# The inverse norms of the attention keys: from diagonal products on TensorE to a transfer through DRAM

## The chip, the core and the metric

The kernel runs on one core of a Trainium2 chip. The metric is the device time of one execution in microseconds (us), the median of several runs. One profiled execution gives the trace. Its engines are PE (TensorE matmul), PEld (its weight loads), DVE (VectorE), ACT (ScalarE), POOL (GpSimd) and SP (SyncE, which here issues the loads and stores). Each engine works through its own instructions in a fixed order.

## What is computed

The reference is one layer with two parallel token mixers. The change sits in the second, latent attention with normed queries and keys:

```python
kv = (_rms(ckv, kv_a_norm) @ w_ukv).reshape(B, T, MLA_HEADS, MLA_NOPE + MLA_V)
k_nope, v = kv[..., :MLA_NOPE], kv[..., MLA_NOPE:]
k = jnp.concatenate([k_nope, broadcast(k_rope)], axis=-1)
k = _rms(k, k_norm)          # each key is divided by the root of its mean square
...
s = jnp.einsum('bqhd,bkhd->bhqk', q, k) * (MLA_QK ** -0.5)
p = jax.nn.softmax(s, axis=-1)
```

There are 8 heads, 512 latent and 256 context tokens, so 768 keys a head. The kernel leaves the keys unscaled in the score product and multiplies each column of the scores by the inverse norm of its key afterwards. For that the 768 inverse norms of a head must stand in every one of the 128 partitions.

## The kernel before

All work on the core is one program whose instructions a scheduler puts in order for each engine; within an engine that order is then fixed. In the stage of interest three strands share the engines. The last part of the first mixer, `gdn_chain(3)`, is a serial recurrence of small 128x128 products (lines L751, L766, L786, L802, L805 on PE, L758 `rho` and L794 `s` on DVE). `queries` and `operands` prepare a head: the products with `ckh`/`ckl`, their splits into a high and a low part (L927 on ACT, L928 on DVE), and transposes (L995, L999, L1007). `attention` computes the scores in eight groups a head: five products of 384 columns into a PSUM bank `d` (L184 to L186, L1034, L1035), of which there are two, then DVE's L1036, which multiplies by `rkb` and takes the row maximum. It empties the bank for the group after next. Then follow exponential, transposes (L1046) and the product with the values.

The operands of a head are computed while an earlier head's attention runs; only heads 0 and 1 (numbered here in order of use) are prepared before any attention. In `operands`, the sum of squares `ssk` of each key ends in L980 on DVE, and POOL raises it to the power -0.5 (`power`, L149): `rk`, 128 partitions x 6 blocks, so that key 128b+p has its inverse norm in partition p, column b. To bring it into all partitions, `rk` is split into two float32r parts (`rkr`: L189 on ACT, L190 on DVE), POOL multiplies the identity by each (`dg`, 128x768, L987), PE multiplies a matrix of ones by both (L1013: two products of 512 and two of 256 columns a head, in two PSUM banks from the rotation of `pbank`), and ACT copies the two banks into `rkb` (L1014).

SP issues the loads in order. The weights (`wchunk`, L177) go through four buffers `wf`, so each load waits until DVE has split an earlier one.

Of the kernel before, what the change touches and what calls it, by code (L numbers as in the profile page):

```python
# [7 lines left out]
F32 = mybir.dt.float32  # L8
F32R = mybir.dt.float32r
AF = mybir.ActivationFunctionType  # L10
ALU = mybir.AluOpType
# [4 lines left out]
P = 128  # L16
# [5 lines left out]
NT = NL + NC  # L22
# [56 lines left out]
def f32(ap):  # L79
    return ap.bitcast(F32)  # L80
# [3 lines left out]
def tile_layer(ctx, tc, I, out, stop=None, dbg=None):  # L84
    nc = tc.nc
    act = nc.scalar
    dve = nc.vector
    pool = nc.gpsimd
    pe = nc.tensor

    def bc(ap, shape):
        return ap.to_broadcast(shape)
# [4 lines left out]
    dr = ctx.enter_context(tc.tile_pool(name="dr", bufs=1, space=DRAM))  # L97
# [3 lines left out]
    def bank(tag):  # L101
        return ps.tile([P, 512], F32, tag=tag, name=tag, bufs=banks[tag])
# [21 lines left out]
    def M(n):  # L124
        lo, hi = MASKS[n]
        return (mk2 if n in EARLY else mk)[:, lo:hi]

    ident = M("ident")
# [15 lines left out]
    onesf = cst.tile([P, P], F32, name="onesf")  # L144
    pool.memset(onesf, 1.0)

    def power(out_ap, in_ap, n, half):
        e = expt[:, 1 if half else 0, 0:n]
        pool.tensor_tensor(out_ap, in_ap, e, ALU.pow)  # L149
# [15 lines left out]
    def wchunk(src, nk=KT, n=P, eng=dve, keep=None):  # L165

        step = min(nk, WN // n)
        res = []
        for k in range(0, nk, step):
            wf = wp.tile([P, WN], F32, tag="wf", name="wf", bufs=4)[:, :step * n]  # L170
            if keep is None:
                wh = wp.tile([P, WN], F32R, tag="wh", name="wh", bufs=3)[:, :step * n]
                wl = wp.tile([P, WN], F32R, tag="wl", name="wl", bufs=3)[:, :step * n]
            else:
                wh = keep.tile([P, WN], F32R, tag="kh", name="kh", bufs=2 * KEEP)
                wl = keep.tile([P, WN], F32R, tag="kl", name="kl", bufs=2 * KEEP)
            nc.sync.dma_start(wf.rearrange("p (k n) -> p k n", k=step), src[:, k:k + step])  # L177
            act.copy(wh, wf)  # L178
            eng.tensor_tensor(wl, wf, f32(wh), ALU.subtract)  # L179
            res += [(wh[:, n * i:n * i + n], wl[:, n * i:n * i + n]) for i in range(step)]  # L180
        return res

    def mm3(po, lh, ll, rh, rl, first, last):
        pe.matmul(po, lh, rh, start=first, stop=False)  # L184
        pe.matmul(po, lh, rl, start=False, stop=False)  # L185
        pe.matmul(po, ll, rh, start=False, stop=last)  # L186

    def split_sb(full, hi, lo):
        act.copy(hi, full)  # L189
        dve.tensor_tensor(lo, full, f32(hi), ALU.subtract)  # L190
# [229 lines left out]
    for b0, n in ((0, 4), (4, 2)):  # L420
        t = bank("t")[:, :128 * n]
# [32 lines left out]
    raw = gx.tile([P, NG + 2 * GAP], F32, name="raw")  # L454
# [439 lines left out]
    lp = lpool.__enter__()  # L894
# [3 lines left out]
    krow = rows[:, 192:384]  # L898
    ropec = rows[:, 384:640].rearrange("p (b n) -> p b n", b=4)
    ropes = rows[:, 640:896].rearrange("p (b n) -> p b n", b=4)  # L900
    onesr = lp.tile([P, P], F32R, name="onesr")
    act.copy(onesr, onesf)
    cqh = lp.tile([P, 3, NL], F32R, name="cqh")
    cql = lp.tile([P, 3, NL], F32R, name="cql")
    ckh = lp.tile([P, 2, NT], F32R, name="ckh")
# [2 lines left out]
    mr = mrpool.__enter__()  # L908
    krx = lp.tile([P, NT], F32R, name="krx")
    for src, th_, tl_, nk, w in ((d_cq, cqh, cql, 3, 128), (d_kv, ckh, ckl, 2, 256)):  # L910
        for c0 in range(0, src.shape[2], w):
            c = slice(c0, c0 + w)
            raw = wp.tile([P, WN], F32, tag="wf", name="raw", bufs=4)[:, :nk * w]
            raw = raw.rearrange("p (a b) -> p a b", a=nk)
            nc.sync.dma_start(raw, src[:, :, c])
            split_sb(raw, th_[:, :, c], tl_[:, :, c])
    raw = mr.tile([P, NT], F32, tag="dg", name="raw")
    nc.sync.dma_start(raw, d_kr)
    act.copy(krx, raw)
    dve.tensor_tensor(krx[64:128], raw[64:128], f32(krx[64:128]), ALU.subtract)  # L920
# [3 lines left out]
    mp = mpool.__enter__()  # L924

    def split_ps(src, hi, lo):
        act.copy(hi, src)  # L927
        dve.tensor_tensor(lo, src, f32(hi), ALU.subtract)  # L928
# [3 lines left out]
    def pbank(pr):  # L932
        turn[0] += 1
        return bank("tece"[turn[0] % 4] if pr else "tdd"[turn[0] % 3])
# [24 lines left out]
    def operands(pr, h, qs, late=False):  # L959
        qn, qr, sc = qs  # L960

        uk = wchunk(I["w_ukv"][2 * pr + h], 2, 256)
        kn = mr.tile([P, 6, P], F32, tag="kn", name="kn", bufs=2)
        v2 = gp.tile([P, 2, 6, P], F32R, tag="A", name="v2", bufs=2)
        ssk = mr.tile([P, 6], F32, tag="ssk", name="ssk", bufs=2)
        rk = mr.tile([P, 6], F32, tag="rk", name="rk", bufs=2)
        junk = mr.tile([P, 128], F32, tag="junk", name="junk2")
        for b2 in range(3):
            po = pbank(pr or late).rearrange("p (a n) -> p a n", a=2)
            for bb in range(2):  # L970
                c = slice(256 * b2 + 128 * bb, 256 * b2 + 128 * bb + 128)
                for k in range(2):
                    mm3(po[:, bb], ckh[:, k, c], ckl[:, k, c], *uk[k], k == 0, k == 1)
            bs = slice(2 * b2, 2 * b2 + 2)
            for bb in range(2):
                act.activation(junk, po[:, bb, 0:128], AF.Square, accum_out=ssk[:, 2 * b2 + bb:2 * b2 + bb + 1])
            split_ps(po[:, :, 128:256], v2[:, 0, bs, :], v2[:, 1, bs, :])
            dve.tensor_tensor(kn[:, bs, :], po[:, :, 0:128], bc(krow[:, 0:128].unsqueeze(1), [P, 2, P]), ALU.mult)
        dve.tensor_tensor(ssk, ssk, sskr, ALU.add)
        dve.tensor_scalar(ssk, ssk, 1.0 / 192, EPS, op0=ALU.mult, op1=ALU.add)  # L980
        power(rk, ssk, 6, False)
        dgs = []
        rks = [mr.tile([P, 6], F32R, tag=t, name="rkr", bufs=2) for t in ("rkh", "rkl")]
        split_sb(rk, *rks)
        for rr, tag in zip(rks, ("dg", "dgl")):
            dg = mr.tile([P, 6, P], F32R, tag=tag, name="dg")
            pool.tensor_tensor(dg, bc(ident.unsqueeze(1), [P, 6, P]), bc(f32(rr).unsqueeze(2), [P, 6, P]), ALU.mult)  # L987
            dgs.append(dg.rearrange("p a b -> p (a b)"))
        qh = mp.tile([P, NL], F32R, tag="qh", name="qh", bufs=2)
        ql = mp.tile([P, NL], F32R, tag="ql", name="ql", bufs=2)  # L990
        qrh = mp.tile([P, NL], F32R, tag="qrh", name="qrh", bufs=2)
        qrl = mp.tile([P, NL], F32R, tag="qrl", name="qrl", bufs=2)
        t = pbank(pr or late)
        for b in range(4):
            pe.transpose(t[:, 128 * b:128 * b + 128], qn[:, b, h, 0:128], ident)  # L995
        split_ps(t, qh, ql)
        t = pbank(pr or late)
        for b in range(4):
            pe.transpose(t[:, 128 * b:128 * b + 128], qr[:, h, b].rearrange("p a b -> p (a b)"), ident)  # L999
        split_ps(t, qrh, qrl)  # L1000
        kh = mp.tile([P, NT], F32R, tag="kh", name="kh", bufs=2)
        kl = mp.tile([P, NT], F32R, tag="kl", name="kl", bufs=2)
        for b0, n in ((0, 4), (4, 2)):
            c = slice(128 * b0, 128 * (b0 + n))
            t = pbank(pr or late)[:, :128 * n]
            for b in range(n):
                pe.transpose(t[:, 128 * b:128 * b + 128], kn[:, b0 + b, :], ident)  # L1007
            split_ps(t, kh[:, c], kl[:, c])
        rkb = mp.tile([P, NT], F32, tag="rkb", name="rkb", bufs=2)
        for b0, n in ((0, 4), (4, 2)):  # L1010
            t = pbank(pr or late)[:, :128 * n]
            for i, dg in enumerate(dgs):
                pe.matmul(t, onesr, dg[:, 128 * b0:128 * (b0 + n)], start=(i == 0), stop=(i == 1))  # L1013
            act.copy(rkb[:, 128 * b0:128 * (b0 + n)], t)  # L1014
        return qh, ql, qrh, qrl, kh, kl, rkb, v2[:, 0], v2[:, 1], sc

    def attention(pr, h, ops):
# [35 lines left out]

    qs = queries(0)
    o0 = operands(0, 0, qs)
    o1 = operands(0, 1, qs, True)
    attention(0, 0, o0)
    gdn_out(3, res3)
    with ahead():
        qs = queries(1)  # L1060
        o0 = operands(1, 0, qs)
# [313 lines left out]
```

## Time and profile before

| | us |
|---|---|
| median of 3 runs (1328.95 to 1334.19) | 1329.18 |
| the profiled execution | 1332.53 |
| its span in the trace | 1330.7 |

A row of the timeline gives start and duration in us, engine, line, operation, tile written `<-` tiles read, the shape, how many in a row, and in brackets how long the engine sat idle before it and what it waited for. "q" behind an engine's name (SPq, ACTq) is its sequencer issuing a transfer. The row of a window gives its length, then, for PE, PEld, DVE, ACT and POOL in this order, the busy time and the number of instructions, then TensorE's granted clock as a share of its full speed, the share of DMA engine time in use and GB/s. Matmuls overlap in the pipeline, so what one costs is the step from its start to the next one's start, and not its duration.

### The profile page before, as it was taken

The page shows a single profiled execution, that of the slowest core. Times are in us where ns is not written, and L with a number is a line of the kernel's source. Part 1 is how long each engine was busy: PE and PEld are TensorE (multiplying, and loading weights), DVE is VectorE, ACT ScalarE, POOL GpSimd, SP SyncE. Part 2 cuts the span into 40 slices and gives each one's busy share as a digit, 9 for nine tenths or more (in the row PEclk, how much of TensorE's full clock was granted, in tenths as well). Part 3 has the DMA queues.
Part 4 walks back from the last instruction along what each step waited for, and adds up shares of the span by engine and source line. Part 5 has one row for each costly group of instructions (what it writes and reads, how often), then busy time and mean ns, then how long its engine had stood idle before and what let it go on. Part 6 is the DMA issues. An engine that isn't in the chain of part 4 may idle for free.

```text
span 1330.7 us, 21029 instructions
## 1 busy us (share of the span) xinstructions
PE 1269.9 (95%) x7430; PEld 1112.8 (84%) x7430; DVE 867.2 (65%) x1861; ACT 648.2 (49%) x1666; POOL 278.5 (21%) x372
## 2 busy tenths in 40 slices
PE   5899899998999999989999999999999999999998
PEld 4798787887888888879899998888997888888886
DVE  4656798866688678747778788676885333333332
ACT  4557575336653675356667576323443242242331
POOL 0022423223410431113112221222041010010110
PEclk9999998988999999999999999999999999999999
DMA  9333225210233124441011013766452222222232
GB/s 359 112 110 88 56 71 128 94 41 9 88 103 104 49 76 120 123 143 60 14 46 37 9 40 131 266 209 249 173 177 95 95 95 95 95 96 95 96 112 86
DMA packets 97993, 141.20 MB, mean 106 GB/s; under 512 B 32736, under 2 KB 41952, under 8 KB 97760
## 3 DMA queue, kind: packets, MB, share of 16 engines
q1 hardware_dynamic: 68576, 127.27, 28.8%
q10 hardware_dynamic: 29312, 12.59, 3.8%
q8 instruction: 59, 0.97, 0.3%
q14 instruction: 46, 0.38, 0.1%
HBM read 124.23 MB, written 15.60 MB: 105 GB/s over the span
## 4 chain that ended last, share of the span: by engine, by line
PE 82%; DVE 7%; DMA 4%; ACT 4%; issue 1%; POOL 1%; SPq 0%; DVEq 0%; ACTq 0%; POOLq 0%
PE d L184 20%; PE d L185 20%; PE d L186 20%; DMA wm<-in_w_mod 2%; PE p L184 1%; PE c L766 1%; PE p L185 1%; PE p L186 1%; PE c L786 1%; PE p L1046 1%; PE c L751 1%; PE e L802 1%; DVE kT L471 1%; PE e L805 1%; PE t L487 1%
## 5 line engine op out<-in xcount | busy, mean ns | idle before, releaser
L178 ACT CAST wh<-wf 128x512 fp32r<-128x512 f32 (+2 forms) x292 | 177.1, 610 | 352.2 <-PE d L185 307.4
L179 DVE TENSOR_TENSOR wl<-wf,wh 128x512 fp32r<-128x512 f32 (+2 forms) x268 | 182.9, 686 | 164.2 <-ACT wh L178 161.5
L184 PE MATMUL d<-hTh,wh 128*128 128x512 f32 x384 | 156.2, 407 | 4.2 <-ACT raw L466 3.5
L185 PE MATMUL d<-hTl,wh 128*128 128x512 f32 x384 | 155.0, 404 | 0.0
L186 PE MATMUL d<-hTh,wl 128*128 128x512 f32 x384 | 154.0, 401 | 0.0
L184 PE MATMUL d<-ah,wh 128*128 128x512 f32 x256 | 100.7, 395 | 0.0
L185 PE MATMUL d<-al,wh 128*128 128x512 f32 x256 | 100.7, 395 | 0.0
L186 PE MATMUL d<-ah,wl 128*128 128x512 f32 x256 | 100.6, 395 | 0.0
L1233 POOL TENSOR_TENSOR a<-r 128x512 f32<-128x512 f32 (+1 forms) x36 | 37.1, 1033 | 269.2 <-ACT r L1231 264.8
L184 PEld LDWEIGHTS d<-hTh,wh 128*128 128x128 f32 x384 | 73.7, 192 | 19.8 <-ACT raw L466 5.0
L186 PE MATMUL d<-h2h,wl 128*128 128x512 f32 x224 | 87.4, 390 | 0.9 <-DVE wl L179 0.9
L185 PE MATMUL d<-h2l,wh 128*128 128x512 f32 x224 | 87.2, 389 | 0.0
L184 PE MATMUL d<-h2h,wh 128*128 128x512 f32 x224 | 87.2, 389 | 0.0
L186 PEld LDWEIGHTS d<-hTh,wl 128*128 128x128 f32 x384 | 73.7, 192 | 14.0
L185 PEld LDWEIGHTS d<-hTl,wh 128*128 128x128 f32 x384 | 73.9, 193 | 13.3
L179 POOL TENSOR_TENSOR wl<-wf,wh 128x512 fp32r<-128x512 f32 x24 | 36.2, 1510 | 133.3 <-ACT wh L178 133.3
L1272 DVE SCALAR_TENSOR_TENSOR x<-d,mcol,x 128x512 f32<-128x512 f32 x32 | 24.0, 751 | 61.5 <-PE d L186 61.5
L186 PEld LDWEIGHTS d<-ah,wl 128*128 128x128 f32 x256 | 48.1, 188 | 11.6
L184 PEld LDWEIGHTS d<-ah,wh 128*128 128x128 f32 x256 | 48.1, 188 | 11.5
L185 PEld LDWEIGHTS d<-al,wh 128*128 128x128 f32 x256 | 48.1, 188 | 11.5
L186 PEld LDWEIGHTS d<-h2h,wl 128*128 128x128 f32 x224 | 42.0, 188 | 10.1 <-DVE wl L179 1.4
L184 PEld LDWEIGHTS d<-h2h,wh 128*128 128x128 f32 x224 | 42.0, 188 | 8.7
(552 smaller groups left out, 3468.0 us busy)
## 6 DMA issues: line engine op xcount, KB each, us to landing
wf<-in_w_mi SPq DMA_DIRECT2D x64, 256.0 KB, 2.7
wf<-in_w_mo SPq DMA_DIRECT2D x64, 256.0 KB, 2.6
wf<-in_w_qkv SPq DMA_DIRECT2D x48, 256.0 KB, 2.8
wm<-in_w_mod SPq DMA_DIRECT2D x40, 256.0 KB, 5.4
wm<-in_w_mod SPq DMA_DIRECT2D x16, 512.0 KB, 9.0
wf<-in_w_gate SPq DMA_DIRECT2D x32, 256.0 KB, 2.7
wms<-in_w_mod SPq DMA_DIRECT2D x12, 512.0 KB, 8.5
wf<-in_w_z SPq DMA_DIRECT2D x16, 256.0 KB, 2.7
```

What stands on the lines that cost most here:

```text
L178: act.copy(wh, wf)
L179: eng.tensor_tensor(wl, wf, f32(wh), ALU.subtract)
L184: pe.matmul(po, lh, rh, start=first, stop=False)
L185: pe.matmul(po, lh, rl, start=False, stop=False)
L186: pe.matmul(po, ll, rh, start=False, stop=last)
L471: dve.scalar_tensor_tensor(dst, raw[:, o + i:o + i + n], convh[:, ch, i:i + 1], dst, ALU.mult, ALU.add)
L487: pe.transpose(t[:, 128 * q:128 * q + 128], src[:, c:c + 128], ident)
L751: pe.matmul(t[:, 0, h, :], kT[:, h, at(bs[d]):at(bs[d]) + 128], S_[d][:, h, :], start=True, stop=True)
L766: pe.matmul(t[:, 0, h, :], Em[d][:, h, :], rho[d][h], start=True, stop=True)
L786: pe.matmul(t[:, 0, h, :], kn[:, h, bs[d], :], y2[d][:, h, :], start=True, stop=True)
L1233: pool.tensor_tensor(a_, r, r, ALU.mult)
L1272: dve.scalar_tensor_tensor(x1[:, ot, :], po, mcol[:, 5, ot, 0:1], x1[:, ot, :], ALU.mult, ALU.add)
```

## The change

The split of `rk`, the two diagonal matrices, the four products and the two copies of each head are gone, with the matrix `onesr`. In their place SP writes `rk` to a small DRAM tensor, transposed, so that the 768 values lie in a row, and then reads this row into all 128 partitions. The tile `raw`, which shared a buffer with `dg`, has a buffer of its own name.

```diff
-    onesr = lp.tile([P, P], F32R, name="onesr")
-    act.copy(onesr, onesf)
...
-        dgs = []
-        rks = [mr.tile([P, 6], F32R, tag=t, name="rkr", bufs=2) for t in ("rkh", "rkl")]
-        split_sb(rk, *rks)
-        for rr, tag in zip(rks, ("dg", "dgl")):
-            dg = mr.tile([P, 6, P], F32R, tag=tag, name="dg")
-            pool.tensor_tensor(dg, bc(ident.unsqueeze(1), [P, 6, P]), bc(f32(rr).unsqueeze(2), [P, 6, P]), ALU.mult)
-            dgs.append(dg.rearrange("p a b -> p (a b)"))
+
+        d_rk = dr.tile([6, P], F32, tag="d_rk", name="d_rk", bufs=2)
+        nc.sync.dma_start(d_rk.rearrange("b p -> p b"), rk, allow_slow_non_contiguous=True)
+        rkb = mp.tile([P, NT], F32, tag="rkb", name="rkb", bufs=2)
+        nc.sync.dma_start(rkb, bc(d_rk.rearrange("b p -> (b p)").unsqueeze(0), [P, NT]))
...
-        rkb = mp.tile([P, NT], F32, tag="rkb", name="rkb", bufs=2)
-        for b0, n in ((0, 4), (4, 2)):
-            t = pbank(pr or late)[:, :128 * n]
-            for i, dg in enumerate(dgs):
-                pe.matmul(t, onesr, dg[:, 128 * b0:128 * (b0 + n)], start=(i == 0), stop=(i == 1))
-            act.copy(rkb[:, 128 * b0:128 * (b0 + n)], t)
```

The scheduler then orders the whole attention stage anew; before and behind it the order is as it was. Lines behind the change move up: L978 is L976, L980 is L978, L1007 is L1003, L1034 and L1035 are L1024 and L1025, L1036 is L1026, and the two transfers are L982 and L984. On SP the two transfers of each head stand among the weight loads; this is the difference for the first two pairs of heads (`in_w_uq` and `in_w_ukv` are weights of `queries` and `operands`):

```order
-L177 DMA wf<-in_w_uq 128x384 x3
+L177 DMA wf<-in_w_uq 128x384
+L982 DMA d_rk<-rk 128x6x1
+L984 DMA rkb<-d_rk 128x768
+L177 DMA wf<-in_w_uq 128x384
+L982 DMA d_rk<-rk 128x6x1
+L984 DMA rkb<-d_rk 128x768
+L177 DMA wf<-in_w_uq 128x384
 L177 DMA wf<-in_w_ukv 128x512 x2
```

Each write waits on SP behind one weight load, and the read waits for the write; the next weight load stands behind both.

On DVE, this is what stands between the last split of head 0's keys (`kl`) and its first product with `rkb` before the change:

```order
L928 TENSOR_TENSOR kl<-d,kh 128x256
L772 TENSOR_SCALAR y_6603<-c,bkd 128x128
L190 TENSOR_TENSOR rkr<-rk,rkr 128x6
L794 SCALAR_TENSOR_TENSOR s_6615<-s_6549,egl,c 128x128 x2
L813 TENSOR_TENSOR ob<-ob,e 128x2x128
L794 SCALAR_TENSOR_TENSOR s_6618<-s_6552,egl,c 128x128 x2
L758 SCALAR_TENSOR_TENSOR rho<-c,negc,vn 128x128 x4
L813 TENSOR_TENSOR ob<-ob,e 128x2x128
L772 TENSOR_SCALAR y_6663<-c,bkd 128x128
L1036 ISA pp,mx<-d,rkb 128x384
```

And this is the same place of the changed program:

```order
L926 TENSOR_TENSOR kl<-d,kh 128x256
L772 TENSOR_SCALAR y_6603<-c,bkd 128x128
L794 SCALAR_TENSOR_TENSOR s_6615<-s_6549,egl,c 128x128 x2
L813 TENSOR_TENSOR ob<-ob,e 128x2x128
L794 SCALAR_TENSOR_TENSOR s_6618<-s_6552,egl,c 128x128 x2
L1026 ISA pp,mx<-d,rkb 128x384
L1026 ISA mx 128x1
L758 SCALAR_TENSOR_TENSOR rho<-c,negc,vn 128x128 x2
L1026 ISA pp,mx<-d,rkb,mx 128x384
L1026 ISA mx 128x1
L758 SCALAR_TENSOR_TENSOR rho<-c,negc,vn 128x128 x2
```

The first product with `rkb` has moved ahead of four steps `rho` of the recurrence, which now queue behind it.

On PE, the program before went from the transposes of head 0's keys straight to the recurrence, and to its first score group, like this (`dg` are the diagonal matrices):

```order
L1007 MATMUL d<-mk,kn 128x128 x6
L766 MATMUL c<-rho,Em 128x128 x2
L802 MATMUL e<-s_6549,qT 128x128 x2
L805 MATMUL e<-y,Qm 128x128
L786 MATMUL c<-y_6597,kn 128x128 x2
L805 MATMUL e<-y,Qm 128x128
L786 MATMUL c<-y_6603,kn 128x128 x2
L751 MATMUL c<-s_6615,kT 128x128 x2
L1013 MATMUL t<-dg,onesr 128x512
L1013 MATMUL d<-dg,onesr 128x256
L184 MATMUL d<-kh,qh 128x384
```

In the changed program twelve products for head 1 (`ckh`, `ckl`; the last of them stands in the first row) come between, and the first score group comes sooner:

```order
L186 MATMUL t<-wh,ckl 128x256
L766 MATMUL c<-rho,Em 128x128 x2
L802 MATMUL e<-s_6549,qT 128x128 x2
L184 MATMUL d<-kh,qh 128x384
L185 MATMUL d<-kl,qh 128x384
L186 MATMUL d<-kh,ql 128x384
L1024 MATMUL d<-krx,qrh 128x384
L1025 MATMUL d<-krx,qrl 128x384
L805 MATMUL e<-y,Qm 128x128
L786 MATMUL c<-y_6597,kn 128x128 x2
L805 MATMUL e<-y,Qm 128x128
L184 MATMUL d<-kh,qh 128x384
```

Two score groups and the products for head 1 thus stand ahead of the third group, the first that needs a bank back from DVE.

## Rows read from the trace of the kernel before

**Rows 1.** The page: span, and busy time of the engines.

```profile
span 1330.7 us, 21029 instructions
PE 1269.9 (95%) x7430; PEld 1112.8 (84%) x7430; DVE 867.2 (65%) x1861; ACT 648.2 (49%) x1666; POOL 278.5 (21%) x372
```

**Rows 2.** Windows: the attention stage's first 10 us and the stage.

```profile
620.00:630.00 10.00, 8.64 (x64) 7.53 (x64) 7.29 (x25) 4.69 (x16) 6.14 (x8) 1.00 0.06 18
620.00:825.00 205.00, 195.70 (x1387) 185.62 (x1387) 159.92 (x482) 135.93 (x417) 47.26 (x38) 1.00 0.11 36
```

**Rows 3.** The stage's window for L1013 alone (PE, PEld), then L1014 alone (ACT).

```profile
620.00:825.00 205.00, 9.95 (x32) 5.41 (x32) 1.00 0.11 36
...
620.00:825.00 205.00, 7.09 (x16) 1.00 0.11 36
```

**Rows 4.** Timeline of PE around the last products of head 2's `rkb`.

```profile
692.45 0.39 PE L1013 MATMUL c<-dg,onesr 128*128 128x512 f32 x1
692.68 0.28 PE L1013 MATMUL e<-dg,onesr 128*128 128x256 f32 x1
692.79 0.33 PE L1035 MATMUL d<-krx,qrl 128*128 128x384 f32 x1
```

**Rows 5.** What PE waited for at L1013, and who waited for L1014.

```profile
  POOL dg L987: 0.6, 2
...
PE c L487 <- ACT rkb L1014: 0.6, 1, 0.6
```

**Rows 6.** Timeline, heads 0, 1, 2: POOL's `rk`, ACT's second copy into `rkb`.

```profile
622.38 1.32 POOL L149 TENSOR_TENSOR rk<-ssk,expt 128x6 f32<-128x6 f32 x1 [1.64 <-DVE ssk L980]
629.68 0.38 ACT L1014 COPY rkb<-d 128x256 f32<-128x256 f32 x1
654.84 1.32 POOL L149 TENSOR_TENSOR rk<-ssk,expt 128x6 f32<-128x6 f32 x1 [16.70 <-DVE ssk L980]
663.81 0.38 ACT L1014 COPY rkb<-c 128x256 f32<-128x256 f32 x1
685.33 1.32 POOL L149 TENSOR_TENSOR rk<-ssk,expt 128x6 f32<-128x6 f32 x1 [7.08 <-DVE sm L1041]
693.36 0.38 ACT L1014 COPY rkb<-e 128x256 f32<-128x256 f32 x1
```

**Rows 7.** DMA issues: KB each, median us from issue to landing.

```profile
wf<-in_w_ukv SPq DMA_DIRECT2D x8, 256.0 KB, 2.9
d_kv<-nres SPq DMA_DIRECT2D x6, 128.0 KB, 2.2
dA<-Da ACTq DMA_DIRECT2D x4, 192.0 KB, 3.0
rows<-in_rows SPq DMA_DIRECT2D x1, 448.0 KB, 3.1
d_kr<-krt SPq DMA_DIRECT2D x1, 384.0 KB, 4.3
raw<-d_kr SPq DMA_DIRECT2D x1, 384.0 KB, 5.4
```

**Rows 8.** Timeline of ACT's queue: a write to DRAM and the read that waits for it.

```profile
151.13 0.39 ACTq L600 DMA_DIRECT2D dA<-Da  x1
153.76 0.36 ACTq L610 DMA_DIRECT2D pt<-dA  x1
```

**Rows 9.** Timeline of SP and POOL: the weight load ahead of head 5, its `rk`.

```profile
744.33 0.33 SPq L177 DMA_DIRECT2D wf<-in_w_bg  x1
745.48 1.32 POOL L149 TENSOR_TENSOR rk<-ssk,expt 128x6 f32<-128x6 f32 x1 [8.63 <-PE d L1035]
```

**Rows 10.** Timeline of DVE ahead of head 0's first L1036.

```profile
625.61 0.60 DVE L794 SCALAR_TENSOR_TENSOR s<-s,egl,c 128x128 f32<-128x128 f32 x2
628.52 0.61 DVE L758 SCALAR_TENSOR_TENSOR rho<-c,negc,vn 128x128 f32<-128x128 f32 x2 [1.80 <-PE c L751]
629.82 0.56 DVE L1036 CUSTOM_DVE_ANT_0 pp<-d,rkb 128x384 f32<-128x384 f32 x1
```

More of the change, by code (lines that the diff above doesn't have):

```diff
@@ L916, in tile_layer @@
             split_sb(raw, th_[:, :, c], tl_[:, :, c])
-    raw = mr.tile([P, NT], F32, tag="dg", name="raw")
+    raw = mr.tile([P, NT], F32, tag="raw", name="raw")
     nc.sync.dma_start(raw, d_kr)
```

## The prediction

> **What bounds the kernel now.** I read the page first: PE is busy for 95% of the span, DVE for 65%, ACT and POOL for less [rows 1]. An average over the whole program says little about one stage, so the windows came next. In the attention stage, from 620 to 825 us, PE is busy for 195.7 of 205 us at full clock, DVE for 159.9, ACT for 135.9 and POOL for 47.3 [rows 2]. PE sets the time there. What it does less is gained, as long as it finds work; what another engine does less is gained only where PE waits for it, and there are just 9.3 us of idle PE to win back (205 - 195.7). 1.36 of these lie in the first 10 us, where head 0's keys get ready [rows 2]. Third, I took the timeline of each head from `rk` to `rkb`, and last the transfers of the same size, since the change puts a transfer into that path.
>
> **What is removed on PE.** Each of 8 heads loses four products, 32 in all. Their window says 9.95 us [rows 3], but that counts pipelined durations. By the steps from start to start, the 512-column product of 692.45 holds PE for 0.23 us and the 256-column one behind it for 0.11 [rows 4]. Sixteen of each give 16 x (0.23 + 0.11) = **5.4 us**. PE also waited 0.6 us for `dg` and 0.6 us for ACT to empty a bank of `rkb` [rows 5]; both waits lose their cause: **1.2 us**.
>
> **What is removed elsewhere.** ACT loses 7.1 us of copies [rows 3], POOL its 16 diagonals, DVE eight tiny splits. None of the three is the bound, so I count nothing for them; what covers this is PE, which is busy meanwhile. If ACT's relief shortens waits of PE, it does so out of the 8.1 us of idle time that are left (9.3 - 1.2). That is a rival below.
>
> **What is added: the path from `rk` to `rkb`.** Before, it ran from the end of POOL's `rk` to the end of ACT's second copy. Head 0: 622.38 + 1.32 = 623.70 to 629.68 + 0.38 = 630.06, so 6.4 us. In the same way 8.0 us for head 1 (656.16 to 664.19) and 7.1 for head 2 (686.65 to 693.74) [rows 6]. Heads 4 and 6 repeat head 2. These five have their first use close behind; heads 3, 5 and 7 have more time.
>
> Now it is a write, a wait, and a read. No data transfer of the trace writes 4-byte pieces, so the write is bounded by others. `d_kv` writes 256 pieces of 512 bytes and lands in 2.2 us; `dA` writes 1536 pieces of 128 bytes (128 partitions x 12 columns) and lands in 3.0 [rows 7]. From the issue of `dA` to that of the read that waits for it there are 153.76 - 151.13 = 2.6 us [rows 8]. Here there are 768 pieces, between the two, and I take 2.6 to the issue of the read; the slowest write in the list, `d_kr`, took 4.3. The read brings 128 rows of 3 KB, 384 KB: 256 KB take 2.9, 448 KB take 3.1, but `raw<-d_kr`, which has exactly this shape, took 5.4 [rows 7]. I take 3.5, nearer to the first two, because the transfers of this stage are few (0.11 of the DMA engines' time, [rows 2]). That all 128 rows come from the same 3 KB of DRAM occurs nowhere before; it is the part that I know least. Sum: 2.6 + 3.5 and about 0.1 to wake SP is **6.2 us**; ends: 2.2 + 2.9 = 5.1 and 4.3 + 5.4 = 9.7. Against 6.4, 8.0 and 7.1 before, `rkb` comes no later than it did.
>
> A rule of the Trainium skill speaks against this write: "DMA: Bandwidth & Descriptors", section "Rules for kernel authors", says that a strided last dimension becomes one descriptor per element, and that transposing by a plain DMA with a rearranged access pattern is 19 times worse than the hardware's transpose. The rows above show no such price down to 128 bytes: 1280 pieces more cost 0.8 us. If each 4-byte piece nonetheless cost 19 times that, 768 of them would take 9 us (an estimate from that page's factor); the five close heads would be late by some 8 us each, and at full price the kernel would take about 1329 + 40 - 7 = 1362 us.
>
> **SP's queue.** The write waits on SP for `rk`, and the read for the write; weight loads queue behind for about 2.7 us. They are issued far ahead of their use, so this costs nothing. The other way round, the write must not wait behind a weight load that has no free buffer. The closest case before is 744.33 for the load against 746.80 for the end of `rk` [rows 9]: 2.5 us of room. DVE's new order keeps the same number of weight splits ahead of each head's sums, so I count nothing. If that cover went, the head would be late by what the load is late.
>
> **The new order.** Head 0 is where it can cost. DVE finishes `s` at 626.21, and its next instruction is now the product with `rkb` [rows 10], which at 623.70 + 6.2 = 629.9 starts as it did before (629.82). DVE stands still for 3.7 us, against 1.80 before. Behind it queue the four `rho` of the recurrence, of which the first two had run at 626.12; PE's L766 waits for them, so the recurrence is set back by up to 4 us. PE itself has two score groups and the twelve products for head 1 to do meanwhile, and would have done those later anyway. By the time the bank comes free it is ahead in attention and behind in the recurrence. Between nothing and the 3.7 us I take **1 us** of PE time lost, nearer to nothing because of that work. Head 1's first product with `rkb` also stands only a few splits behind its sums, and I take **1 us** for it too. Later heads have more PE work ahead of the group that needs a bank: nothing.
>
> **Sum.** -5.4 - 1.2 + 1 + 1 = **-4.6 us**. Against its own execution, that is 1332.53 - 4.6 = 1327.9. That execution lies 3.35 us above the median of the runs (1329.18), so the forecast is 1329.2 - 4.6 = **1324.6 us**. A measurement of this kernel can tell a change of about 0.5%, 6.6 us, from none.
>
> **Rivals.**
> - *The gain is used up* (1329, from 1327 to 1335). DVE waits for `rkb` at five heads, and PE runs dry behind it. If each is late by 1.3 us at full price, 5 x 1.3 = 6.5 us eat the 5.4 + 1.2. For it: the two bounds of the path differ by 4.6 us, and the first use followed the copies at once. Against: 6.2 is below what the path took before.
> - *More is gained* (1320.6). ACT's 7.1 us go out of the stage in which PE's splits, exponentials and bank copies wait for it, and half of the 8.1 us of other idle time closes: -4.6 - 4 = -8.6. Against: the new order was not made by these waits, and DVE still does 150 us or more of work.
> - *The transfer is slow* (1340, slower). The 4-byte pieces or the 128 reads of one row take what the two `d_kr` transfers took, 9.7 us. Then the path is 3.5 us longer than forecast at each of five close heads: 17.5 us at full price, less 6.6: +10.9. It decides from about 2.7 us of lateness a head on, a path of some 9 us. The page's 19-fold rule is the same mechanism at a higher price. For it: no row shows such pieces. Against: pieces of 128 bytes were cheap.
> - *The change does nothing on PE*, because the products had filled idle time: 1329, counted with the first. PE's 95% in this stage speaks against it.
>
> **Chances.** The forecast (1322.6 to 1327) has 0.36, the gain used up 0.21, more gained 0.28, the slow transfer 0.15. Faster by over 0.5% is therefore 0.28, within 0.5% 0.36 + 0.21 = 0.57, slower 0.15. The range leaves out the slow case and a little of the best: 1316 to 1336. The forecast's own range is 1322.6 to 1327, on the fast side of no change.
>
> **What would show it.** In the changed kernel's profile: PE's busy sum in the stage falls by about 10 us in durations, while the stage's length falls by 4 to 5. `d_rk` lands in 2.2 to 3 us and `rkb` in 3 to 4. DVE waits for the transfer at its first product with `rkb` of heads 0 and 1 for 2 to 4 us, and at later heads for 2 or less. The weight loads behind the transfers are on time. The prediction is wrong if `rkb` lands over 8 us after `rk`, if a write sits behind a weight load, or if PE's idle time in the stage changes by more than 4 us either way.

## The result and the profile after

The changed kernel takes 1380.02 us (median of 6 runs, 1377.56 to 1384.53), the kernel before on the same chip 1330.12: a ratio of 1.0374, with a 95% interval of 1.0349 to 1.0399. The change costs 50 us where 4.6 were to be gained. The prediction was wrong.

The page of the changed kernel, its span, engines and clock in 40 slices, to set beside [rows 1]:

```profile
span 1381.4 us, 20968 instructions
PE 1277.1 (92%) x7398; PEld 1117.2 (81%) x7398; DVE 865.3 (63%) x1853; ACT 641.1 (46%) x1641; POOL 254.6 (18%) x356
...
PEclk9999999999999999988899898999999999999999
```

PE has 32 products fewer and is yet busy for 7.2 us longer than before; the share of the span falls from 95% to 92%. Each digit of the clock's row stands for 34.5 us. The first 8 lies ahead of the attention stage and is not the change's doing: the kernel before has a stretch of half clock at the same place, as a window of its trace shows (its clock, 0.53, is the third figure from the end):

```profile
593.30:603.60 10.30, 8.54 (x34) 7.95 (x34) 6.01 (x12) 4.84 (x10) 0.41 (x1) 0.53 0.68 220
```

The other digits of 8 lie in the attention stage, where the kernel before had full clock [rows 2].

The transfers, and what the queue of SP and DVE waited for between 600 and 890 us (us in total, times, longest), beside [rows 7]:

```profile
d_rk<-rk SPq DMA_DIRECT2D x8, 3.0 KB, 10.2
rkb<-d_rk SPq DMA_DIRECT2D x8, 384.0 KB, 4.0
...
SPq L984 <- DMA d_rk<-rk: 76.8, 8, 11.0
...
DVE pp L1026 <- DMA rkb<-d_rk: 56.6, 7, 13.1
```

The smallest transfer of the program, 3 KB, is the slowest of these: it lands after 10.2 us, and the read of 384 KB behind it after 4.0. DVE stands still for it at seven of the eight heads. The path of head 0, on POOL, SP, DVE and PE, beside [rows 6] and [rows 10]:

```profile
623.05 1.32 POOL L149 TENSOR_TENSOR rk<-ssk,expt 128x6 f32<-128x6 f32 x1 [1.64 <-DVE ssk L978]
624.40 0.38 SPq L982 DMA_DIRECT2D d_rk<-rk  x1
635.29 0.33 SPq L984 DMA_DIRECT2D rkb<-d_rk  x1
638.82 0.56 DVE L1026 CUSTOM_DVE_ANT_0 pp<-d,rkb 128x384 f32<-128x384 f32 x1 [10.44 <-DMA rkb<-d_rk]
639.44 0.69 PE L184 MATMUL d<-kh,qh 128*128 128x384 f32 x1 [9.92 <-DVE mx L1026]
```

SP issues the write as soon as `rk` is there, the read 10.9 us later, and DVE starts 3.5 us behind that: 14.4 us from the end of `rk` (624.37), where it was 6.1 before (629.82 - 623.70, [rows 6, 10]). PE has filled both banks, and its third score group waits for 9.9 us. At the last head it is the same, as the chain that ended last shows (start, length, what):

```profile
842.90 10.12 DMA d_rk<-rk
853.03 5.00 DMA rkb<-d_rk
858.17 0.56 DVE pp L1026
858.79 0.69 PE d L184
```

What the DMA engines do meanwhile tells a window of head 0's write (length, then busy time and instructions of PE, PEld, DVE, ACT and POOL, the clock, the DMA share, GB/s):

```profile
626.00:635.30 9.30, 3.52 (x29) 3.33 (x27) 1.63 (x5) 1.25 (x4) 0.81 (x2) 0.96 0.02 1
```

They are busy for 2% of the time. The pieces are not waiting in a crowd of transfers, and no bandwidth is short; their landing is late. The packets of the trace narrow down where the time goes. A window from 625.20 to 625.90 us holds all packets of this write, 784 of 4 bytes (the 768 pieces and 16 more), and from there to 635.20 us SP's and ACT's transfers have none. A kernel shown below writes the same pieces 64 bytes apart; its write is issued at 624.36 us and its packets fill the same window. The two windows, of the changed kernel and of that one:

```profile
DMA packets 784, 0.00 MB, mean 4 GB/s; under 512 B 784, under 2 KB 784, under 8 KB 784
```

```profile
DMA packets 784, 0.00 MB, mean 4 GB/s; under 512 B 784, under 2 KB 784, under 8 KB 784
```

There the read could be issued at 627.17 us, here at 635.29. So by these records the DMA engines are done with the pieces equally soon in both, and the late write loses its time after that. What happens to the pieces then, no trace shows.

### The profile page after: what moved, and what is told of

The parts are those of the page before. It is cut to its first block, busy times and chain, and to the rows that moved or that the text cites. A ratio compares the mean times of both kernels' runs of the same rounds, so it can differ in the third digit from the quotient of the medians.

```text
span 1381.4 us, 20968 instructions
## 1 busy us (share of the span) xinstructions
PE 1277.1 (92%) x7398; PEld 1117.2 (81%) x7398; DVE 865.3 (63%) x1853; ACT 641.1 (46%) x1641; POOL 254.6 (18%) x356
## 5 line engine op out<-in xcount | busy, mean ns | idle before, releaser
L184 PE MATMUL d<-kh,qh 128*128 128x384 f32 x64 | 27.1, 426 | 49.1 <-DVE mx L1026 48.8
L1026 DVE CUSTOM_DVE_ANT_0 pp<-d,rkb 128x384 f32<-128x384 f32 x32 | 17.7, 552 | 61.6 <-DMA rkb<-d_rk 56.6
```

The lines of the kernel that those rows point to most:

```text
L1026: dve.tensor_tensor_reduce(sx[:, ks], s, rkb[:, ks], 1.0, mx[:, 0:1] if kk else -3.0e38, ALU.mult, ALU.max, accum_out=mx[:, kk:kk + 1])
```

## The experiments

Three theories stood after the result. **A**: the write of 4-byte pieces lands late, and everything else follows. **B**: the new order of the engines costs the time. **C**: the 128 reads of one 3 KB row are slow.

Executions that are alike up to the attention stage reach it up to 13 us apart (head 0's `rk` begins between 611 and 624 us in the kernels below). So, beside the times, I compare what lies between the start of head 0's `rk` and the end of the span, in one execution of each kernel. It is 1330.7 - 622.38 = **708.3 us before** [rows 1, 6] and 1381.4 - 623.05 = **758.4 us after**: the 50 us lie there. Two kernels further below keep the diagonal products and add writes that nobody reads; they have 1326.3 - 616.36 = 709.9 and 1322.8 - 613.00 = 709.8 us, so the measure repeats within some 1.6 us. (Where the order ahead of `rk` differs a little, in the kernels with 512-byte pieces and with pieces 64 bytes apart, the mark itself may stand a little earlier.)

### 24-byte pieces

Each partition writes its six norms as one piece. The row then has them in another order, so the scores are multiplied by the norms of other keys; the order of all engines is that of the changed kernel.

```diff
-        d_rk = dr.tile([6, P], F32, ...)
-        nc.sync.dma_start(d_rk.rearrange("b p -> p b"), rk, ...)
+        d_rk = dr.tile([P, 6], F32, ...)
+        nc.sync.dma_start(d_rk, rk)
```

> As the changed kernel, but the inverse norms go to DRAM in their own order, six neighbours of a partition in one piece of 24 bytes: 128 pieces in place of 768. The read is the same 3 KB row; the values come back in another order, so the keys are scaled by the wrong norms. The order of PE, DVE, ACT and POOL is that of the changed kernel, row by row. Theory A (the write of 768 pieces of 4 bytes is what costs, about 10 us until it lands): the write lands in 3 us or less, DVE's wait at the first product with the row falls from 56.6 us in all to under 15, and the time to 1325 to 1335 us. Rival B (the new order of the stage, in which PE and DVE stand in each other's way): the order is unchanged, so the time stays above 1365. Rival C (the broadcast read of one row, 4.0 us, or its queueing): the write may get faster, but the time stays above 1350.

Measured: 1318.66 us (8 runs, 1313.38 to 1323.66), ratio 0.9925 (0.9898 to 0.9951). Its transfers, DVE's wait, and PE's wait for the bank:

```profile
d_rk<-rk SPq DMA_DIRECT2D x8, 3.0 KB, 1.4
rkb<-d_rk SPq DMA_DIRECT2D x8, 384.0 KB, 3.6
...
DVE pp L1026 <- DMA rkb<-d_rk: 6.3, 3, 3.1
...
PE d L184 <- DVE mx L1026: 1.6, 3, 0.7
```

The time lies below the 1325 to 1335 that were expected. The same bytes in 128 pieces land in 1.4 us. Behind the write the same read takes 3.6 us, and the same order is not slow but 0.8% below the kernel before. B and C fall.

Since the order is the same, the loss can be split up. These are the windows from the end of head 0's `kv` products to the last score group of head 7, of the changed kernel and then of this one:

```profile
617.20:870.60 253.40, 200.96 (x1351) 189.84 (x1350) 156.28 (x470) 127.12 (x395) 25.25 (x23) 0.90 0.15 41
```

```profile
609.40:805.20 195.80, 190.01 (x1353) 179.42 (x1350) 156.02 (x470) 126.94 (x395) 24.88 (x23) 1.00 0.18 53
```

The stretch is 57.6 us longer. PE's idle time is 52.4 us against 5.8: 46.6 of them. The same products take PE 200.96 us against 190.01: the other 11.0. The idle time is the wait for the bank that DVE has not emptied, which in the changed kernel is

```profile
PE d L184 <- DVE mx L1026: 48.8, 6, 10.3
```

against 1.6 us here. The slower products are a matter of the clock. PE went idle, its granted clock fell to half, 1.2 GHz, during the wait, and stayed there for some us after it was over; the changed kernel's timeline shows both levels, ahead of head 0's wait and behind it:

```profile
624.64 0.34 PE L185 MATMUL d<-kl,qh 128*128 128x384 f32 x1
624.82 0.35 PE L186 MATMUL d<-kh,ql 128*128 128x384 f32 x1
625.00 0.34 PE L1024 MATMUL d<-krx,qrh 128*128 128x384 f32 x1
...
639.93 0.52 PE L185 MATMUL d<-kl,qh 128*128 128x384 f32 x1
640.25 0.52 PE L186 MATMUL d<-kh,ql 128*128 128x384 f32 x1
640.57 0.52 PE L1024 MATMUL d<-krx,qrh 128*128 128x384 f32 x1
...
634.63:644.87 10.24, 5.43 (x20) 5.43 (x21) 3.07 (x13) 2.00 (x5) 0.43 (x2) 0.50 0.14 38
```

A step from product to product is 0.18 us there and 0.32 here, and the last row is the stretch of half clock (0.50). Its first half is the wait, its second half work at half speed.

### 512-byte pieces

PE transposes `rk` in one product and ACT copies the 6 rows out of PSUM, so that the write has 6 pieces of 512 bytes. The keys get their own norms, as in the changed kernel.

```diff
+        t = pbank(pr or late)[0:6, 0:P]
+        pe.transpose(t, rk, ident)
+        rkt = mr.tile([6, P], F32, tag="rkt", name="rkt", bufs=2)
+        act.copy(rkt, t)
-        nc.sync.dma_start(d_rk.rearrange("b p -> p b"), rk, ...)
+        nc.sync.dma_start(d_rk, rkt)
```

> PE transposes the 128x6 norms of a head in one product (6 x 128 in a PSUM bank), ACT copies them, and the write has 6 pieces of 512 bytes; the read is that of the changed kernel, and so is the result. Theory A: the write lands in about 2.2 us and the read in 4, with the transpose and the copy about 8 us from the norms to the row, where the products took 6.4 to 8.0. PE keeps nearly all of the 5.4 us of products that the change took away, so the time is 1322 to 1332 us, close to the kernel before. Rivals B and C: above 1350.

Measured: 1321.87 us (12 runs, 1315.56 to 1328.37), ratio 0.9946 (0.9918 to 0.9974). The read and DVE's wait:

```profile
rkb<-d_rk SPq DMA_DIRECT2D x8, 384.0 KB, 4.2
...
DVE pp L1030 <- DMA rkb<-d_rk: 4.0, 3, 2.4
```

From head 0's `rk` to the end it is 1313.9 - 611.02 = 702.9 us. One product and one small copy a head take the loss away: the version is far faster than the changed kernel and 0.5% below the kernel before, a small gain whose interval ends below 1.

### Is it the number of pieces, their size, or their place?

Two kernels keep 768 pieces and change one thing each. In the first POOL repeats every norm 16 times, so that each piece fills 64 bytes; in the second each piece is 4 bytes and goes to a 64-byte stretch of its own. What is read into `rkb` is then not the 768 norms.

```diff
+        rk16 = mr.tile([P, 6, 16], F32, ...)
+        pool.tensor_copy(rk16, bc(rk.unsqueeze(2), [P, 6, 16]))
-        d_rk = dr.tile([6, P], F32, ...)
-        nc.sync.dma_start(d_rk.rearrange("b p -> p b"), rk, ...)
+        d_rk = dr.tile([6, P, 16], F32, ...)
+        nc.sync.dma_start(d_rk.rearrange("b p n -> p b n"), rk16)
```

> Each inverse norm is repeated 16 times on POOL and written as a whole piece of 64 bytes: again 768 pieces, at the same transposed places, none of them sharing 64 bytes of DRAM with another. The read takes 3 KB of that tensor, so the keys are scaled by the wrong norms. If the number of pieces is what costs, the write lands in about 10 us as before and the time stays near 1380. If it is the smallness of the pieces or that 16 of them share 64 bytes of DRAM, it lands in 3 us or less and the time is 1325 to 1340.

```diff
+        d_rk = d_rks[(2 * pr + h) % 2]
+        nc.sync.dma_start(d_rk.rearrange("b p n -> p b n")[:, :, 0:1], rk.unsqueeze(2), ...)
```

> Each inverse norm is written as a piece of 4 bytes, 768 pieces, but each to a 64-byte stretch of DRAM of its own (two tensors filled with ones ahead of the stage; the read takes 3 KB of one of them, so most keys are scaled by one). If pieces of 4 bytes are slow wherever they land, the write takes about 10 us and the time stays near 1380. If what costs is that neighbouring pieces share a stretch of DRAM, it lands in 3 us or less and the time is 1325 to 1345.

Measured: 1327.49 and 1329.7 us (one profiled run each; the kernel before had 1327.79 beside them), and from head 0's `rk` to the end 1325.8 - 624.21 = 701.6 and 1326.9 - 623.01 = 703.9. The writes of the one and of the other:

```profile
d_rk<-rk SPq DMA_DIRECT2D x8, 48.0 KB, 2.0
...
d_rk<-rk SPq DMA_DIRECT2D x8, 3.0 KB, 2.4
```

768 pieces are not slow, and neither are pieces of 4 bytes. Both are fast where each has 64 bytes of DRAM to itself. Two more kernels, run once each, show how the landing goes with the place: the kernel before with an extra write of `rk` for each head that nobody reads, every head in another layout, and the same with the heads in the opposite order.

```diff
+        if hd == 0:
+            dt = dr.tile([6, P], F32, name="d_s4")
+            nc.sync.dma_start(dt.rearrange("b p -> p b"), rk, ...)
+        elif hd == 1:
+            dt = dr.tile([6, P, 2], F32, name="d_s8")
+            nc.sync.dma_start(dt.rearrange("b p n -> p b n")[:, :, 0:1], rk.unsqueeze(2), ...)
...
```

> The kernel before, which keeps its diagonal products, with one more write of rk from SP for each head that nobody reads, each in another layout in DRAM. In order of the heads: the transposed one of the change (pieces of 4 bytes, 4 bytes apart), the same 8, 16, 32 and 64 bytes apart, one column alone (128 pieces side by side), the untransposed order with 4-byte pieces 8 bytes apart, and three columns. The time should be that of the kernel before within 0.5%, since nobody waits. Theory A1 (what is slow is that pieces from several partitions fall in the same 64 bytes, and each must wait for the one before): with 16, 8, 4, 2 and 1 partitions to 64 bytes the landing falls step by step, about 10, 6, 4, 3, 2.4 us; one column alone is as slow as all six if it is the depth at one place that counts, or about a sixth of the extra if it is the count of such pieces; the untransposed order, whose pieces in 64 bytes come from two partitions at most, lands in under 3 us. Rival A2 (any 4-byte piece in a line that is not its own is slow, whoever shares it): the untransposed order is as slow as the transposed one, and 8 to 32 bytes apart stay near 10 us.

> The eight extra writes that nobody reads, added to the kernel before, with the heads in the opposite order: the first head in use writes three columns, the last the transposed layout of the change. If the landing belongs to the layout and not to the head or its moment, each comes within 1 us of what it took the other way round (4 bytes apart 11.7, 8 bytes 4.8, 16 bytes 3.1, 32 bytes 2.4, 64 bytes 2.8, one column 7.6, untransposed 8 bytes apart 4.8, three columns 8.8). If it belongs to the moment (other transfers under way), the values change places or spread. The time stays that of the kernel before within 0.5%.

| layout of the 4-byte pieces | pieces | in 64 bytes | landing, us |
|---|---|---|---|
| 4 bytes apart (the change) | 768 | 16 | 11.7, 8.6 |
| the same, three columns | 384 | 16 | 8.8, 8.3 |
| the same, one column | 128 | 16 | 7.6, 6.8 |
| 8 bytes apart | 768 | 8 | 4.8, 4.6 |
| 8 bytes apart, untransposed | 768 | 8 | 4.8, 5.1 |
| 16 bytes apart | 768 | 4 | 3.1, 2.8 |
| 32 bytes apart | 768 | 2 | 2.4, 2.5 |
| 64 bytes apart | 768 | 1 | 2.8, 2.4 |

The first row of the table in the two traces, as the view of one line gives it:

```profile
L985 SPq DMA_DIRECT2D d_s<-rk x1: 383/383/383, 617.7 to 617.7; - x1
DMA to landing us min/median/max: 11.7/11.7/11.7
```

```profile
L985 SPq DMA_DIRECT2D d_s<-rk x1: 378/378/378, 791.2 to 791.2; - x1
DMA to landing us min/median/max: 8.6/8.6/8.6
```

With nobody waiting these kernels took 1328.11 and 1324.55 us (one run each; before 1329.91 and 1331.45): no cost of the writes alone shows (the second lies 0.52% below, where 0.5% was expected, and within the range of the kernel before). The landing follows the layout and not the head, within 0.8 us but for the first row (11.7 against 8.6; in the changed kernel the time from write to read went from 8.6 to 11.4 as well). It rises steeply as the pieces come closer together than 16 bytes, and hardly before that. The column of 64 bytes is one way to count that: with 32 bytes it would read 8, 4, 2, 1 and 1, which fits the equal landings at 32 and 64 bytes apart as well, so how large the stretch is that pieces share stays open. 128 pieces, a sixth, still take from 65 to 79% of the time, so what counts is mostly how close they lie, and less how many there are. Two more expectations missed: the first row moved by more than 1 us, and the untransposed order, in which at most two partitions share 64 bytes, is as slow as the transposed one at the same spacing. So whose pieces they are makes no difference that shows.

### Does anything else of the write cost time?

The first kernel takes the wait away: the read brings a row that already lies in DRAM. The slow write is issued all the same, and the norms are left out of the scores. (By the starts in the traces some 160 of PE's products, 90 instructions of DVE and 40 of ACT stand at other places in the order than in the changed kernel.)

```diff
-        nc.sync.dma_start(rkb, bc(d_rk.rearrange("b p -> (b p)").unsqueeze(0), [P, NT]))
+        nc.sync.dma_start(rkb, bc(I["rows"][0, 0:NT].unsqueeze(0), [P, NT]))
```

> The changed kernel, but the read into rkb takes a row of an input that already lies in DRAM, so it waits for no write; the slow write is still issued, nobody reads what it wrote, and the keys' norms are left out of the scores. Theory A (the write's landing, 10 to 11 us a head, is what costs): DVE waits for rkb under 3 us in all, the span is 1311 to 1318 us and the time 1315 to 1322, as with 24-byte pieces; a further gain over that run of up to 5 us is what the remaining 6.3 us of waits there are worth. Rival D (the write disturbs by its 768 pieces also where nobody waits for it, by holding the SP queue or the DMA engines): over 1335 us.

Measured: 1324.64 us (10 runs, 1317.88 to 1328.23), ratio 0.9955 (0.993 to 0.998); from head 0's `rk` to the end 1326.5 - 624.05 = 702.5 us. DVE no longer waits for `rkb`. Its two transfers:

```profile
rkb<-in_rows SPq DMA_DIRECT2D x8, 384.0 KB, 7.4
d_rk<-rk SPq DMA_DIRECT2D x8, 3.0 KB, 9.5
```

The write is as slow as in the changed kernel, and the time that it cost is gone. The time lies 2.6 us above what was expected, and the stretch 2.8 us above the one with 24-byte pieces (699.7): the further gain from taking the last 6.3 us of DVE's wait away isn't there; the changed order, which this run does not separate, may hide it. The reads take 7.4 us here at the median, twice as long as elsewhere. Some of them are issued right behind a slow write, but that can't be the only reason: the first two are issued at 598.8 and 599.3 us, 26 us ahead of the first slow write, and take 7.8 us. Why was not tried.

The other two kernels turn it round: a late `rkb` without small pieces that share a place. One passes the 24-byte rows through five more DRAM tensors, the other writes them 96 times over. Both keep the order of the norms of the kernel with 24-byte pieces. The scheduler changed the order of the engines in both, more than was expected: against the changed kernel some 370 of PE's products, 170 instructions of DVE and 100 of ACT stand elsewhere with five transfers, and 290, 150 and 80 with 96 copies.

```diff
+        for k in range(5):
+            d_nx = dr.tile([P, 6], F32, tag="d_nx%d" % k, ...)
+            nc.sync.dma_start(d_nx, d_rk)
+            d_rk = d_nx
```

> The kernel with 24-byte pieces, but the norms go from one DRAM tensor to the next five times before the read, each transfer waiting for the one before: no small pieces, only a late rkb, about as late as in the changed kernel (five times about 1.7 us, 8 to 11 us more). The engines' order changes a little, since the scheduler sees the longer chain. Theory A (lateness alone makes the time, through DVE's wait, PE's idle time and the half clock behind it): 1365 to 1395 us, with DVE waiting 45 to 65 us for rkb and TensorE's granted clock falling to 0.5 in the stage as in the changed kernel. Rival E (the small pieces also disturb other transfers or PE, and lateness is only part of the loss): under 1355 us at the same lateness.

```diff
+        d_rk = dr.tile([96, P, 6], F32, ...)
+        nc.sync.dma_start(d_rk.rearrange("k p b -> p k b"), bc(rk.unsqueeze(1), [P, 96, 6]), ...)
```

> The kernel with 24-byte pieces, but the write brings each norm 96 times to DRAM (12288 pieces of 24 bytes, 288 KB, no two of them over one another), and the read takes the first copy: a late rkb by sheer number of pieces, with only one write and one read on SP, so that the order of the engines stays nearer to that of the changed kernel than with five transfers in a row. From 768 pieces in 2.0 us and 1536 in 3.0 it should land in some 8 to 14 us. Theory A (lateness alone): at a landing of 10 us DVE waits 45 to 65 us for rkb, TensorE's clock falls to 0.5 behind the waits, and the time is 1365 to 1395 us; each us of landing less or more takes 6 to 8 us off or adds them. Rival E (the small pieces that share 64 bytes cost something beside lateness): at a landing of 10 us the time is under 1360.

Measured: 1353.79 us (4 runs, 1351.52 to 1361.43; ratio 1.0192, 1.0144 to 1.0239) and 1445.39 us (5 runs, 1435.36 to 1447.67; ratio 1.0876, 1.0826 to 1.0926). Five transfers:

```profile
DVE pp L1026 <- DMA rkb<-d_nx: 23.3, 6, 5.8
```

96 copies:

```profile
d_rk<-rk SPq DMA_DIRECT2D x8, 288.0 KB, 23.0
...
DVE pp L1026 <- DMA rkb<-d_rk: 108.8, 8, 18.4
...
605.84:921.96 316.12, 204.27 (x1352) 193.85 (x1350) 156.54 (x470) 126.27 (x395) 23.65 (x23) 0.83 0.90 40
```

Both misses first. With five transfers the time came out where the rival wanted it, but DVE waited only 23.3 us. From the end of `rk` to the first product with `rkb` it is 14.6 us or more at every head, as in the changed kernel, but in the order that the scheduler made for this kernel DVE has other work for most of that, so it isn't the comparison that was meant. It shows something else: a row as late as in the changed kernel costs 33.2 us against the 24-byte pieces in this order and 58.7 in that of the changed kernel (both worked out below). How much lateness costs is a matter of what DVE has to do ahead of the wait. With 96 copies the write took 23 us and not 8 to 14, and it keeps the DMA engines busy for 0.90 of the stage, which the changed kernel does not. What the two give is the price of a wait. From head 0's `rk` to the end it is 699.7 us with 24-byte pieces (1315.0 - 615.28), 758.4 in the changed kernel and 821.9 with 96 copies (1433.6 - 611.70). The changed kernel has 56.6 - 6.3 = 50.3 us of wait more than the first and takes 58.7 longer, 1.17 us for each; with 96 copies it is 102.5 and 122.2, 1.19 us for each. Five transfers, in an order with more differences, give 17.0 and 33.2 (1352.0 - 619.06 = 732.9), 1.95. For each us of the write's landing it is (821.9 - 758.4) / (23.0 - 10.2) = 5.0 us, a little under the 6 to 8 expected. A wait costs no more with the small pieces than without them. That the busy DMA engines of the 96 copies cost PE something beside the wait can be ruled out for the most part: of its 316.12 - 204.27 = 111.9 us of idle time in the stage, this is the wait for the bank:

```profile
PE d L184 <- DVE mx L1026: 106.5, 11, 17.6
```

In the window of the 96 copies, further above, the clock (0.83 over the stage) shows the same half speed behind the waits without any small piece. So lateness is all that the write costs, as far as these runs can tell.

## Why the prediction was wrong

- **The step that failed** is the write's term in "What is added: the path from `rk` to `rkb`": "I take 2.6 to the issue of the read". It was bounded by writes of 512 and 128 bytes, 2.2 to 4.3 us [rows 7], and measured 8.6 to 11.4 us, 10.9 at head 0. The rows had no piece below 128 bytes, and none that shares 64 bytes of DRAM with another. By size and number the argument held: 768 pieces of 4 bytes, each in its own 64 bytes, land in 2.4 us. What it left out was the place, that is how close together the pieces lie, which no row showed. The prediction's own sign of being wrong, `rkb` over 8 us after `rk`, came true at every head.
- **The read** was right: 3.5 us forecast, 4.0 measured, and 3.5 at head 0. That 128 reads take one row of 3 KB, named as the least known part, does not make it slow.
- **The saving** was right in its size: where the write is quick, the stretch from head 0's `rk` on is 4.4 to 8.6 us shorter than before (703.9 with 4-byte pieces apart, 699.7 with 24-byte pieces, against 708.3), forecast 5.4 + 1.2 = 6.6 before the new order was paid and 4.6 behind it. No run separates the products' saving from the price of the order.
- **The new order** shows no cost of its own where `rkb` comes in time; whether the forecast 2 us for heads 0 and 1 were spent is open. With `rkb` late the `rho` queue behind DVE's wait as the prediction said, and they set PE's recurrence back too (L758 at 639.30 against 628.52 before, [rows 10]).
- **SP's queue** was right: the write went out 0.02 to 0.04 us after `rk` at every head, and ACT, which takes the weights first, waits for no load of `wf` between 600 and 880 us.
- **How many heads** was wrong: five were called close. From the end of `rk` to the first product it is now 13.8 to 15.3 us at every head, and DVE waited at seven. A wait at one head also makes the next one late: the sums of head 3's keys queue on DVE behind its wait for head 2, and its `rk` starts 20.9 us after that of head 2 (728.26 - 707.33), where it is 13.3 us with 24-byte pieces.
- **The slow transfer**, the rival at 0.15, was right in kind and place ("the 4-byte pieces"). It gave 1340 us, and 1380 were measured. Its price was too low by its path, 9.7 us for 14.4, by two more heads, and by the clock, which was not in it at all: 11.0 of the 57.6 us are products at half speed behind the waits. The stretch measured 46.6 + 11.0 = 57.6 us more than with 24-byte pieces, which themselves gain 8.6 on the kernel before: 49.0 lost, and the times differ by 50.
- **The rule that spoke against the write** had the direction, and I set it aside because pieces of 128 bytes were cheap. It is in the Trainium skill, "DMA: Bandwidth & Descriptors", "Rules for kernel authors": transposing by a rearranged access pattern is 19 times worse than the hardware's transpose. The estimate from it, 9 us for the write, lies near the 10.2 measured, but by luck: it multiplied a price for each piece, and the same 768 pieces of 4 bytes, one descriptor each, land in 2.4 us at 64 bytes apart. (Nor do 9 us make a head late by 8: the path would be 9 + 3.5 + 0.1 = 12.6 us against 6.4 to 8.0 before.) The Trainium skill's page "DMA: Bandwidth & Descriptors", "Specifications", also says that below 512 bytes the DMA engine does a read-modify-write. That alone is not slow here, as pieces of 24 and 64 bytes land in 1.4 and 2.0 us; whether it is what makes close pieces late, no run shows.

## What to carry to other kernels

A row of a larger piece says nothing about a smaller one that shares its place in memory: before a transposing write goes into a path that something waits for, make its pieces whole rows, here with one product on PE. (Pieces 32 bytes apart land as fast, but what it costs to read them back into a row was not measured.) A wait behind which PE runs dry costs more than its length, because the clock stays at half for a while afterwards (1.17 us for each us here). How much of a late operand becomes a wait is a matter of the order: with other work ahead of it on DVE the same lateness cost 33 us in place of 59. To see whether a transfer or the new order is at fault, change the transfer's layout alone and keep the order; and when whole executions drift, compare from a mark just ahead of the change.

## What the runs showed of the hardware

- 768 pieces of 4 bytes land in DRAM in 8.6 to 11.7 us when they lie 4 bytes apart, 4.6 to 5.1 at 8 bytes, 2.8 to 3.1 at 16, 2.4 to 2.8 at 32 or 64; 128 pieces 4 bytes apart take 6.8 to 7.6. The trace has all packets of such a write within 0.7 us, whether it lands early or late, and the DMA engines are idle for the rest (0.02 of their time).
- 128 partitions reading the same 3 KB row of DRAM take 3.1 to 5.4 us where the read waits for the write (3.4 to 4.2 at the median), no more than another load of this size (`raw<-d_kr`, 5.4 [rows 7]). In the kernel where it doesn't wait it took 7.4 at the median, and why is open.
- TensorE's granted clock was at half (0.50) from 634.63 to 644.87, of which the last 5 us were work; before, the whole stage had full clock [rows 2].
